# Weight, activation and S slots of a two-block transformer kernel moved to other byte places in SBUF

## The chip, the cores and the metric

The kernel runs on one core of one Trainium2 chip. The metric is the device time of one execution in microseconds (us); of several runs the median is given.

## What is computed

Two transformer blocks run one after the other on one sequence of 256 tokens, D = 1024, in fp32. The first has two layers, a differential attention and a stick-breaking attention, each followed by a sparse "PEER" layer. The second has four layers (sparse-index attention, sliding window, latent attention, sparse-index attention), each followed by an MLP with squared ReLU. What matters here is the PEER layer and the MLP:

```python
def _peer(x, w_pq, sub_keys, u, v):
    ...
    q = (xt @ w_pq).reshape(T, PEER_HEADS, 2, PEER_HALF)
    scores = jnp.einsum('thcd,hckd->thck', q, sub_keys)
    ...
    def block(args):
        xblk, idb, gb = args
        u_sel = jnp.take(u, idb, axis=0)
        h = jax.nn.gelu(jnp.einsum('td,ted->te', xblk, u_sel), approximate=False)
        v_sel = jnp.take(v, idb, axis=0)
        return jnp.einsum('te,ted->td', gb * h, v_sel)

def sqrelu_mlp(h, w_up, w_down):
    return jnp.square(jax.nn.relu(h @ w_up)) @ w_down
```

The 16384 experts are not gathered: the kernel multiplies with all of `u` and all of `v`, and a dense matrix of gates, zero for experts that were not chosen, lies between the two.

## The kernel before

**Chunks.** All weights come as 932 chunks of 128 partitions x 1024 fp32 (4096 bytes a partition), in the order of `stream_plan`. `Stream._load` fetches a chunk into one of three `raw` tiles (a DMA on SP's queue, line 106). `Stream._fill` splits it into two parts: ScalarE writes the rounded high part `whi` (line 134), VectorE, and for some chunks GpSimd, the rest `wlo` (line 136). Activations are split the same way. A product of fp32 precision is then three matmuls: high x high, high x low, low x high, all through the helper `mm` (line 229).

**Places.** A slot's place is its start in bytes within a partition of SBUF. The slots of `whi` and `wlo` come from a base pool with 4 of each, used in turn, and in most stages from a second, lent pool of 5 to 7 of each. A slot has 1040 elements = 4160 bytes, of which 4096 are used, so neighbouring slots differ by 64 bytes modulo 512. The four base slots of `whi` start at bytes 30720, 43200, 39040 and 34880 in the order of use, those of `wlo` at 47360, 59840, 55680 and 51520. Modulo 512 that is (0, 256), (192, 448), (128, 384) and (64, 320) for the pairs (`whi`, `wlo`). The activations `hT` (two tiles of `Parts`, 8192 bytes each) and the S parts share two places, 64000 and 72192, both 0 modulo 512. Inside all of these tiles an operand of a matmul starts at a multiple of 512 bytes from the tile's start, so the two numbers of a pair are the distances, modulo 512, from the activation's operand to the weight's operand.

**The sparse layer** (`peer`, layers 0 and 1). First 128 chunks of `peer_u`: per chunk 24 matmuls of 256 columns into `ps_h` (`fm_products`), with the weights as the stationary operand (`LDWEIGHTS`) and `hT` moving. In the shadow of these, VectorE selects experts (`select`) and TensorE, VectorE and ScalarE build the gates (`gate`, `ps_g`). Then 128 chunks of `peer_v`: per chunk 12 matmuls of 512 columns into `acc` (`acc_rows`), with S parts stationary and the weights moving; `split_s` makes the S parts, one pair of 8192 bytes for four chunks. Chunks of `peer_u` and the first 70 of `peer_v` use base slots alone; later ones a lent pool too.

**The MLPs** (`mlp`, four of them): 32 pairs of an `up` chunk (24 matmuls of 256 columns into `ps_fm`) and a `dn` chunk (12 of 512 into `acc`), with base and lent slots. In the long middle part of an MLP both kinds of chunk lie in the 7 lent slots in turn.

The order of instructions is set by a scheduler that places recorded instructions on each engine. Between the sparse layer and the mixer before it, GpSimd's queue issues three DMAs: two that save `x` to DRAM (`x_dram`, line 737) and one that loads the sub-keys (`peer_keys`, line 774) into the tile `Xb`.

Of the kernel before, what the change touches and what calls it, by code (L numbers as in the profile page):

```python
# [11 lines left out]
F32R = mybir.dt.float32r  # L12
# [7 lines left out]
P = 128  # L20
D = 1024
S = 256
ND = 8
NEG = -1.0e30
SLOT = 1040
ALPHA = 4.0 ** 0.25
LAMBDA_INIT = 0.8 - 0.6 * math.exp(0.0)
N_KEYS = 128
# [55 lines left out]
class Stream:  # L84
# [7 lines left out]
    def __init__(self, tc, plan, find, raw, parts):  # L92
# [5 lines left out]
        self.raws, self.done = {}, {}  # L98
        self.loaded = self.split = self.pos = 0

    def _load(self):
        c = self.loaded
        src = self.find(*self.plan[c])
        n = src.shape[-1]
        t = self.raw_pool.tile([P, 1024], F32, tag="raw", name=f"raw{c}")
        self.nc.sync.dma_start(t[:, :n], src)
        self.raws[c] = (t, n)
        self.loaded += 1
# [7 lines left out]
    def _fill(self, last):  # L116
        last = min(last, len(self.plan) - 1)
        while self.split <= last:
            c = self.split
            pool = self._slot(c)  # L120
            if pool is None:
                return
            pool[2].append(c)
            if c not in self.raws:
                self._load()
            t, n = self.raws.pop(c)
            hi = pool[0].tile([P, SLOT], F32R, tag="whi", name=f"whi{c}")[:, :1024]
            lo = pool[0].tile([P, SLOT], F32R, tag="wlo", name=f"wlo{c}")[:, :1024]
            name, g = self.plan[c]
            lo_eng = self.nc.gpsimd if name in POOL_LO and g in POOL_LO[name] else self.nc.vector  # L130
            if name in DVE_HI:
                self.nc.vector.tensor_copy(hi[:, :n], t[:, :n])
            else:
                self.last_hi = self.nc.scalar.copy(hi[:, :n], t[:, :n])  # L134
            with self.tc.issue_after(self.behind) if self.n_behind and lo_eng is self.nc.vector else nullcontext():
                lo_eng.tensor_tensor(lo[:, :n], t[:, :n], hi[:, :n].bitcast(F32), ALU.subtract)  # L136
            self.n_behind = max(self.n_behind - 1, 0)
            self.done[c] = (hi, lo)
            self.split += 1
            while self.loaded < min(self.split + self.N_RAW, len(self.plan)):  # L140
                self._load()
# [35 lines left out]
def tile_two_blocks(ctx: ExitStack, tc: tile.TileContext, t: dict, out: bass.AP, dbg=None):  # L177
# [5 lines left out]
    xt_pool = ctx.enter_context(tc.tile_pool(name="xt_pool", bufs=2))  # L183
# [53 lines left out]
    class Parts:  # L237


        def __init__(self):  # L240
            self.t = [xt_pool.tile([P, 4, 2, 2, P], F32R, tag="xt", name=f"hT{i}") for i in range(2)]

        def hi(self, d):
            return self.t[d // 4][:, d % 4, :, 0, :]
# [114 lines left out]
    def lend(px, bufs, *names):  # L359

        st.lend(px.enter_context(tc.tile_pool(name="lent", bufs=bufs)), bufs, names)
        px.callback(st.take_back)
# [4 lines left out]
    def new_accs():  # L367
        return [halves(a2.tile([P, 2, 512], F32, tag="a2", name=f"acc{tt}")) for tt in range(2)]
# [290 lines left out]
    def stick_breaking(hT):  # L659
        with ExitStack() as px:  # L660
            k1 = px.enter_context(tc.tile_pool(name="k1", bufs=1))
            sp = px.enter_context(tc.tile_pool(name="sp", bufs=2))
            lend(px, 6, "b_v", "b_kq", "b_wo")
            smask = k1.tile([P, 384], F32, name="smask")
            seg = k1.tile([P, 768], F32, name="seg")
            nc.gpsimd.dma_start(smask, t["k_smask"])
            nc.gpsimd.dma_start(seg, t["k_seg"])
            lng = bcast(k1, t["ln_g"][2], D, "lng")
            lnb = bcast(k1, t["ln_b"][2], D, "lnb")
            v_sb = k1.tile([P, 2, D], F32, name="v_sb")  # L670
            accs = new_accs()
            ch = [(("b_v", d), lambda tt, part, d=d: hT.one(d, tt, part)) for d in range(8)]
            acc_rows(ch[:4], accs, True, 1)
            for d in range(4, 8):
                acc_rows([ch[d]], accs, False, stop=d == 7)
            for tt in range(2):
                nc.scalar.copy(half(v_sb[:, tt], 0), accs[tt][0])
                nc.vector.tensor_copy(half(v_sb[:, tt], 1), accs[tt][1])
            oT = new_oT(k1)
            stt = {}  # L680

            def stage_p(g):
                res = []
                for i in range(2):
                    ps = proj_fm(hT, "b_kq", 2 * g + i)
                    r = sp.tile([P, S], F32, tag=f"raw{i}", name="kq")
                    nc.scalar.copy(r, ps[:, :S])
                    res.append(r)
                stt[g] = res

            def stage_l(g):
                kr, qr = stt.pop(g)
                ps = logits_pair(lambda h: qr[h * 64 : h * 64 + 64, :], lambda h: kr[h * 64 : h * 64 + 64, :])
                z = sp.tile([P, 768], F32, tag="z", name="z")
                zv = z.rearrange("p (a b) -> p a b", a=2)
                nc.vector.scalar_tensor_tensor(
                    zv, ps[:, :, :384], 0.125, smask.unsqueeze(1).to_broadcast([P, 2, 384]), ALU.mult, ALU.add
                )
                e = sp.tile([P, 768], F32, tag="e", name="e")
                nc.scalar.activation(e, z, AF.Abs)  # L700
                nc.scalar.activation(e, e, AF.Exp, scale=-1.0)
                nc.scalar.activation(e, e, AF.Ln, bias=1.0)
                nc.vector.scalar_tensor_tensor(e, z, 0.0, e, ALU.max, ALU.add)
                c = sp.tile([P, 768], F32, tag="c", name="c")
                nc.vector.tensor_tensor_scan(c[:, ::-1], seg[:, ::-1], e[:, ::-1], 0.0, ALU.mult, ALU.add)
                nc.vector.tensor_tensor(z, z, c, ALU.subtract)
                nc.scalar.activation(z, z, AF.Exp)
                stt[g] = zv

            def stage_t(g):  # L710
                zv = stt.pop(g)
                pTs = transposes_pair(zv, sp)
                ps = ms.tile([P, 512], F32, tag="ms", name="ps_av")
                for h in range(2):
                    f = slice(g * P + h * 64, g * P + h * 64 + 64)
                    o = ps[h * 64 : h * 64 + 64]
                    mm(o[:, :S], v_sb[:, 0, f], pTs[:, h, : 2 * P], start=True)
                    mm(o[:, P:S], v_sb[:, 1, f], pTs[:, h, 2 * P :], stop=True)
                pe["behind"] = pe["last"]
                copy_parts(ps[:, :S], g, oT)  # L720

            for s in range(8 + 2):
                if s < 8:
                    stage_p(s)
                if 0 <= s - 1 < 8:
                    stage_l(s - 1)
                if 0 <= s - 2 < 8:
                    stage_t(s - 2)
            nT = Parts()
            acc_wo("b_wo", oT, lambda tt, acc: to_hT(x[:, tt, :], tt, nT, norm_residual(tt, acc, lng, lnb, sp)))  # L730
            return nT


    def peer(layer, hT, last):
# [5 lines left out]
        with ExitStack() as px:  # L740
# [218 lines left out]
            def split_s(b):  # L959
                src = Xa[:, 4 * b : 4 * b + 4, :] if b < NA else Xb[:, 4 * b - J1 : 4 * b - J1 + 4, :]  # L960
                for n in range(2 if b >= NA else 0):
                    hb = ab.tile([P, 2, S], F32, tag="hs", name="hb")
                    nc.gpsimd.dma_start(hb, h_dram[(4 * b - J1) // 2 + n])
                    nc.vector.tensor_tensor(src[:, 2 * n : 2 * n + 2], src[:, 2 * n : 2 * n + 2], hb, ALU.mult)
                if b < NB - 2:
                    sh = xt_pool.tile([P, 2, 4, S], F32R, tag="xt", name="S_parts")
                    hi, lo = sh[:, 0], sh[:, 1]
                elif b == NB - 2:
                    hi, lo = (ab.tile([P, 4, S], F32R, tag="AB", name="S_parts") for _ in range(2))
                else:  # L970
                    hi, lo = (own["k1"].tile([P, 4, S], F32R, name=f"S_last{i}") for i in range(2))
                nc.scalar.copy(hi, src)
                dve_sub_lo(lo, src, hi)
                return [
                    ((f"peer_v{layer}", b * 4 + i), lambda tt, part, i=i: (hi, lo)[part][:, i, tt * P : (tt + 1) * P])
                    for i in range(4)
                ]
# [16 lines left out]
            nT = None  # L994
# [591 lines left out]
    hT = Parts()  # L1586
# [3 lines left out]
    hT = diff_attention(hT)  # L1590
    dump(0)
    hT = peer(0, hT, False)
    dump(1)
    hT = stick_breaking(hT)
    dump(2)
    hT = peer(1, hT, True)
    dump(3)
    mixers = [lambda h: dsa(0, 0, h), lambda h: swa(1, h), lambda h: mla(2, h), lambda h: dsa(1, 3, h)]
    for i in range(4):
        hT = mixers[i](hT)  # L1600
        dump(4 + 2 * i)
        hT = mlp(i, *hT)
# [136 lines left out]
```

## Time and profile before

| | |
|---|---|
| median of 3 runs | 3140.53 us (3134.71 to 3141.01) |
| the profiled execution | 3139.05 us, of which the span of its instructions 3137.3 us |
| TensorE busy | 3023.1 us (96%), mean granted clock 0.984 of full speed |
| VectorE, ScalarE, GpSimd busy | 2081.8, 1666.3, 316.6 us |
| `peer_u` of layer 0, of layer 1 | 206.4 to 627.2, 1157.0 to 1578.0 us |
| `peer_v` of layer 0, of layer 1 | 627.3 to 990.2, 1578.0 to 1943.0 us |
| the four MLPs | 185.8, 187.1, 187.7 and 184.4 us |

A trace lists each instruction with its start. Matmuls are pipelined, so a matmul's own duration (0.28 us for 256 columns) spans several that run behind it; the pace is read from start to start.

### The profile page before, as it was taken

To read this page: it belongs to the slowest core of one execution; us is meant where nothing else is said; L and a number is where in the kernel's file an instruction comes from. 1 tells how busy PE (TensorE), PEld (TensorE's weight loads), DVE (VectorE), ACT (ScalarE), POOL (GpSimd) and SP (SyncE) were. 2 spreads that over 40 slices of the span, in tenths; PEclk is the share of its full clock that TensorE was granted. 3 is DMA by queue.
4 is the path that set the end of the run, shared out by engine and by line. 5 is a ranking of instruction groups with operands and counts; after the bars stand their busy time and mean duration, and the time that the engine had idled before them with its cause. 6 is when DMAs were issued, how large, how long until landed. Compare 5 with 4: busy or idle time off the path is not lost.

```text
span 3137.3 us, 51266 instructions
## 1 busy us (share of the span) xinstructions
PE 3023.1 (96%) x19968; PEld 2720.8 (87%) x19968; DVE 2081.8 (66%) x3603; ACT 1666.3 (53%) x2844; POOL 316.6 (10%) x246
## 2 busy tenths in 40 slices
PE   8699999999999899999999999999999989999999
PEld 6599999978887789999988887889889968998898
DVE  5479867775555769957766555865566566556654
ACT  5434568744443634568744444554555455554553
POOL 1410000010001310000010002400120021003200
PEclk9899999999999999999999999999999999999999
DMA  6855555576655435555576654445526532554364
GB/s 201 134 161 184 184 189 169 169 265 205 223 189 183 146 122 182 180 191 169 169 258 211 229 191 159 150 162 188 184 78 217 189 110 98 194 189 143 125 201 135
DMA packets 157636, 551.05 MB, mean 176 GB/s; under 512 B 18880, under 2 KB 19712, under 8 KB 157392
## 3 DMA queue, kind: packets, MB, share of 16 engines
q1 hardware_dynamic: 135216, 489.42, 47.0%
q0 software_dynamic: 12112, 41.54, 5.3%
q10 hardware_dynamic: 10064, 16.81, 1.5%
q8 instruction: 157, 2.57, 0.3%
q14 instruction: 87, 0.71, 0.1%
HBM read 523.59 MB, written 24.10 MB: 175 GB/s over the span
## 4 chain that ended last, share of the span: by engine, by line
PE 79%; DMA 8%; DVE 5%; ACT 3%; issue 2%; POOL 1%; SPq 0%; ACTq 0%; DVEq 0%; POOLq 0%
PE acc L229 31%; PE ps_h L229 23%; PE ps_fm L229 17%; PE ps_g L229 4%; DMA hb<-h_dram 3%; DVE wlo L136 1%; ACT whi L134 1%; PE ps_av L229 1%; PE ps_l L229 1%; POOL wlo L136 1%; DMA raw<-in_a_wo_dram 1%; DMA raw<-in_dsa_in_dram 1%; DMA raw<-in_peer_q_dram 1%; PE ps_pT L456 1%; DMA raw<-in_b_kq_dram 1%
## 5 line engine op out<-in xcount | busy, mean ns | idle before, releaser
L134 ACT CAST whi<-raw 128x1024 fp32r<-128x1024 f32 (+1 forms) x908 | 948.0, 1046 | 1007.9 <-PE acc L229 279.3
L136 DVE TENSOR_TENSOR wlo<-raw,whi 128x1024 fp32r<-128x1024 f32 (+1 forms) x854 | 1043.0, 1225 | 606.6 <-ACT whi L134 602.7
L229 PE MATMUL ps_h<-hT,whi 128*128 128x256 f32 x4096 | 733.5, 281 | 0.0
L229 PE MATMUL ps_fm<-hT,whi 128*128 128x256 f32 x3424 | 659.9, 286 | 13.5 <-DVE hT L235 4.1
L229 PEld LDWEIGHTS ps_h<-hT,whi 128*128 128x128 f32 x4096 | 628.2, 189 | 1.0
L229 PEld LDWEIGHTS ps_fm<-hT,whi 128*128 128x128 f32 x3424 | 555.1, 191 | 33.1 <-DVE hT L235 5.3
L229 PE MATMUL ps_h<-hT,wlo 128*128 128x256 f32 x2048 | 577.6, 282 | 0.0
L229 PE MATMUL acc<-whi,S_parts 128*128 128x512 f32 x1984 | 539.8, 393 | 0.0
L229 PE MATMUL ps_fm<-hT,wlo 128*128 128x256 f32 (+1 forms) x1936 | 529.3, 283 | 0.0
L229 PEld LDWEIGHTS acc<-whi,S_parts 128*128 128x128 f32 x1984 | 372.6, 188 | 86.0
L229 PEld LDWEIGHTS ps_h<-hT,wlo 128*128 128x128 f32 x2048 | 386.9, 189 | 0.2
L229 PEld LDWEIGHTS ps_fm<-hT,wlo 128*128 128x128 f32 (+1 forms) x1936 | 369.1, 191 | 1.3 <-issue 0.5
L229 PE MATMUL acc<-wlo,S_parts 128*128 128x512 f32 x992 | 310.3, 394 | 4.3 <-DVE wlo L136 4.3
L136 POOL TENSOR_TENSOR wlo<-raw,whi 128x1024 fp32r<-128x1024 f32 (+1 forms) x78 | 196.0, 2524 | 1042.7 <-ACT whi L134 967.1
L229 PEld LDWEIGHTS acc<-wlo,S_parts 128*128 128x128 f32 x992 | 185.8, 188 | 48.8 <-DVE wlo L136 6.3
L229 PE MATMUL acc<-whi,hh 128*128 128x512 f32 x512 | 162.9, 394 | 0.0
L229 PE MATMUL acc<-wlo,hh 128*128 128x512 f32 x512 | 162.6, 393 | 0.0
L229 PE MATMUL acc<-whi,hl 128*128 128x512 f32 x512 | 162.0, 393 | 0.0
L892 DVE TENSOR_SCALAR AB<-iota,selT 128x128 f32<-128x128 f32 x512 | 141.7, 340 | 12.4 <-PE ps_g L229 11.9
L229 PE MATMUL acc<-whi,oT 128*128 128x512 f32 x384 | 128.9, 419 | 11.8 <-ACT oT L482 9.2
L896 ACT ACTIVATE AB<-iota,selT 128x128 f32<-128x128 f32 x384 | 122.9, 391 | 30.0 <-PE ps_g L229 29.4
L229 PE MATMUL ps_g<-AB 128*128 128x128 f32 x1024 | 133.5, 275 | 0.0
(353 smaller groups left out, 3192.7 us busy)
## 6 DMA issues: line engine op xcount, KB each, us to landing
raw<-in_peer_u_dram SPq DMA_DIRECT2D x256, 512.0 KB, 3.7
raw<-in_peer_v_dram SPq DMA_DIRECT2D x256, 512.0 KB, 4.3
raw<-in_up_dram SPq DMA_DIRECT2D x128, 512.0 KB, 4.2
raw<-in_dn_dram SPq DMA_DIRECT2D x128, 512.0 KB, 4.2
raw<-in_dsa_in_dram SPq DMA_DIRECT2D x30, 512.0 KB, 4.2
h_dram<-hs ACTq DMA_DIRECT2D x56, 256.0 KB, 2.2
hb<-h_dram POOLq DMA_DIRECT2D x56, 256.0 KB, 3.7
raw<-in_a_qk_dram SPq DMA_DIRECT2D x16, 512.0 KB, 4.3
```

The lines of the kernel that those rows point to most:

```text
L134: self.last_hi = self.nc.scalar.copy(hi[:, :n], t[:, :n])
L136: lo_eng.tensor_tensor(lo[:, :n], t[:, :n], hi[:, :n].bitcast(F32), ALU.subtract)
L229: pe["last"] = nc.tensor.matmul(o, lhsT, rhs, start=start, stop=stop)
L456: nc.tensor.transpose(pT[:, h, b * P : (b + 1) * P], p_sb[:, h, b * P : (b + 1) * P], ident)
L892: nc.vector.tensor_scalar(A[:, i], iota, selT[:, 0, tk : tk + 1], selT[:, 2, tk : tk + 1], ALU.is_equal, ALU.mult)
L896: nc.scalar.activation(B[:, i], iota, AF.Abs, bias=selT[:, 1, tk : tk + 1], scale=-1.0)
```

## The change

The slots get other places; no instruction is added or taken away.

- A base slot has 1088 elements = 4352 bytes (17 x 256), a lent slot 1024 = 4096 bytes, a tile of `hT` or S 2112 elements = 8448 bytes (33 x 256).
- In `peer_u0` and `peer_v1` the weights of chunk g begin 16 x (g mod 16) bytes into their base slots, `whi` and `wlo` alike.
- The `hT` that the stick-breaking layer leaves for sparse layer 1 begins 64 bytes into its tiles (`Parts(16)`).
- The S parts of group b in `peer_v` of layer 0 begin 16 x (b mod 16) bytes into theirs.
- Everything else that is stationary or moving in these stages starts where its slot starts.

The resulting tiles of `hT` start at bytes 65536 and 73984, 0 and 256 modulo 512. The base slots start at 30720, 43776, 39424 and 35072 (`whi`) and 48128, 61184, 56832 and 52480 (`wlo`): 0, 256, 0 and 256 for both parts. In `peer_u0` the distances of both parts are thus equal, and run through all multiples of 16; in `peer_u1` they are 192 or 448 for both parts in every chunk. In the first three MLPs the lent slots of both parts lie at 128, in the fourth at 0, and `hh`, `hl` lie at the same place modulo 512 as the `dn` weights.

```diff
-SLOT = 1040
+SLIDE = 64
...
+    def slide(self, key):
+
+        name, g = key
+        return 4 * (g % 16) if name in ("peer_u0", "peer_v1") else 0
...
-            hi = pool[0].tile([P, SLOT], F32R, tag="whi", name=f"whi{c}")[:, :1024]
-            lo = pool[0].tile([P, SLOT], F32R, tag="wlo", name=f"wlo{c}")[:, :1024]
+            base = pool is self.pools[0]
+            width = 1024 + (SLIDE if base else 0)
+            at = self.slide(self.plan[c]) if base else 0
+            hi = pool[0].tile([P, width], F32R, tag="whi", name=f"whi{c}")[:, at : at + 1024]
+            lo = pool[0].tile([P, width], F32R, tag="wlo", name=f"wlo{c}")[:, at : at + 1024]
...
-        def __init__(self):
-            self.t = [xt_pool.tile([P, 4, 2, 2, P], F32R, tag="xt", name=f"hT{i}") for i in range(2)]
+        def __init__(self, at=0):
+            whole = [xt_pool.tile([P, 2048 + SLIDE], F32R, tag="xt", name=f"hT{i}") for i in range(2)]
+            self.t = [
+                w[:, at : at + 2048].rearrange("p (d a b t) -> p d a b t", d=4, a=2, b=2) for w in whole
+            ]
...
-            nT = Parts()
+            nT = Parts(16)
             acc_wo("b_wo", oT, lambda tt, acc: to_hT(x[:, tt, :], tt, nT, norm_residual(tt, acc, lng, lnb, sp)))
...
-                    sh = xt_pool.tile([P, 2, 4, S], F32R, tag="xt", name="S_parts")
+                    at = 4 * (b % 16) if layer == 0 else 0
+                    sh = xt_pool.tile([P, 2048 + SLIDE], F32R, tag="xt", name="S_parts")
+                    sh = sh[:, at : at + 2048].rearrange("p (a b t) -> p a b t", a=2, b=4)
```

On TensorE, VectorE, ScalarE and SP the order of the instructions is word for word what it was. On GpSimd one DMA of each sparse layer stands elsewhere. Before, at the start of sparse layer 0 (`Xb` is the tile that takes the sub-keys, `x_dram` the copy of `x` in DRAM, the `wlo` rows split chunks of `peer_q0`):

```order
L136 TENSOR_TENSOR wlo_1426<-raw_1411,whi_1425 128x1024
L136 TENSOR_TENSOR wlo_1432<-raw_1417,whi_1431 128x1024
L774 DMA Xb<-in_peer_keys_dram 128x1024
L737 DMA x_dram<-x 128x1024
L136 TENSOR_TENSOR wlo_1608<-raw_1423,whi_1607 128x1024
L136 TENSOR_TENSOR wlo_1614<-raw_1429,whi_1613 128x1024
L737 DMA x_dram<-x 128x1024
```

And in the changed kernel, at the same place of the same queue:

```order
L144 TENSOR_TENSOR wlo_1426<-raw_1411,whi_1425 128x1024
L144 TENSOR_TENSOR wlo_1432<-raw_1417,whi_1431 128x1024
L748 DMA x_dram<-x 128x1024
L144 TENSOR_TENSOR wlo_1608<-raw_1423,whi_1607 128x1024
L144 TENSOR_TENSOR wlo_1614<-raw_1429,whi_1613 128x1024
L748 DMA x_dram<-x 128x1024
L785 DMA Xb<-in_peer_keys_dram 128x1024
```

The load of the sub-keys now stands behind both saves of `x`; the same happens at the start of sparse layer 1.

## Rows read from the trace of the kernel before

**Rows 1.** The page: busy time by engine, and the chain that ended last.
```profile
PE 3023.1 (96%) x19968; PEld 2720.8 (87%) x19968; DVE 2081.8 (66%) x3603; ACT 1666.3 (53%) x2844; POOL 316.6 (10%) x246
...
PE 79%; DMA 8%; DVE 5%; ACT 3%; issue 2%; POOL 1%; SPq 0%; ACTq 0%; DVEq 0%; POOLq 0%
```

**Rows 2.** Busy time in stretches: `peer_u0`, `peer_v0`, the first MLP.
```profile
core 0: us, PE busy (x) PEld busy (x) DVE busy (x) ACT busy (x) POOL busy (x), PEclk, DMA share, GB/s
206.40:627.20 420.80, 420.80 (x3632) 419.80 (x3630) 346.76 (x822) 267.34 (x469) 0.55 (x1) 1.00 0.54 178
627.30:990.20 362.90, 358.47 (x1545) 290.12 (x1544) 215.30 (x195) 170.88 (x169) 27.51 (x35) 1.00 0.65 215
2058.80:2244.60 185.80, 184.75 (x1193) 167.06 (x1192) 114.91 (x144) 98.62 (x150) 10.60 (x5) 1.00 0.59 193
```

**Rows 3.** Timeline of PE in `peer_u0`: the first matmuls of five chunks on end.
```profile
294.34 0.40 PE L229 MATMUL ps_h<-hT,whi 128*128 128x256 f32 x2
...
297.22 0.39 PE L229 MATMUL ps_h<-hT,whi 128*128 128x256 f32 x2
...
299.94 0.39 PE L229 MATMUL ps_h<-hT,whi 128*128 128x256 f32 x2
...
302.78 0.40 PE L229 MATMUL ps_h<-hT,whi 128*128 128x256 f32 x2
...
305.52 0.40 PE L229 MATMUL ps_h<-hT,whi 128*128 128x256 f32 x2
```

**Rows 4.** Timeline of PE in `peer_v0`: the first low-part matmuls of five chunks.
```profile
666.64 0.62 PE L229 MATMUL acc<-wlo,S_parts 128*128 128x512 f32 x2
...
669.39 0.63 PE L229 MATMUL acc<-wlo,S_parts 128*128 128x512 f32 x2
...
672.18 0.63 PE L229 MATMUL acc<-wlo,S_parts 128*128 128x512 f32 x2
...
674.97 0.62 PE L229 MATMUL acc<-wlo,S_parts 128*128 128x512 f32 x2
...
677.73 0.39 PE L229 MATMUL acc<-wlo,S_parts 128*128 128x512 f32 x1
```

**Rows 5.** Timeline of PE in the first MLP: an `up`, a `dn`, and later `up` chunks.
```profile
2142.83 0.41 PE L229 MATMUL ps_fm<-hT,whi 128*128 128x256 f32 x2
...
2145.67 0.62 PE L229 MATMUL acc<-whi,hh 128*128 128x512 f32 x2
...
2148.45 0.28 PE L229 MATMUL ps_fm<-hT,whi 128*128 128x256 f32 x1
...
2182.11 0.41 PE L229 MATMUL ps_fm<-hT,whi 128*128 128x256 f32 x2
```

**Rows 6.** Timeline of PE in the first attention: one chunk of `a_qk`, first and last.
```profile
80.45 0.40 PE L229 MATMUL ps_fm<-hT,whi 128*128 128x256 f32 x2
...
83.17 0.28 PE L229 MATMUL ps_fm<-hT,wlo 128*128 128x256 f32 x1
```

**Rows 7.** The tile `whi`: durations in ns, min/median/max, of the two splitting instructions.
```profile
L134 ACT CAST whi<-raw x908: 822/1049/1061, 7.0 to 3114.3; 128x1024 fp32r<-128x1024 f32 x180, 128x832 fp32r<-128x832 f32 x1, 128x768 fp32r<-128x768 f32 x1
L136 DVE TENSOR_TENSOR wlo<-raw,whi x854: 949/1224/2524, 8.1 to 3115.4; 128x1024 fp32r<-128x1024 f32 x170, 128x768 fp32r<-128x768 f32 x1
```

**Rows 8.** Timeline of POOL: the second saves of `x`; then the sub-keys' landing times.
```profile
183.28 0.56 POOL L737 DMA_DIRECT2D x_dram<-x  x1 [1.50 <-DVE x L401]
...
1133.97 0.57 POOL L737 DMA_DIRECT2D x_dram<-x  x1 [1.51 <-DVE x L401]
...
DMA to landing us min/median/max: 4.1/4.6/5.1
```

**Rows 9.** Timeline of PE: the first readers of the sub-keys, layers 0 and 1.
```profile
195.52 0.49 PE L229 MATMUL ps_sc<-Xb 64*128 64x128 f32 x2
...
1146.22 0.48 PE L229 MATMUL ps_sc<-Xb 64*128 64x128 f32 x2
```

## The prediction

> **What bounds the kernel now.** I read the page first: TensorE is busy 96% of the span and holds 79% of the chain that ended last [rows 1]. [...] So the question is whether the pace depends on where the operands lie, which only the timeline tells.
>
> It does. Five chunks of `peer_u0` on end run the same 24 matmuls on the same `hT`, and start 2.88, 2.72, 2.84 and 2.74 us apart [rows 3]. Their slots are, in that order, (0, 256), (192, 448), (128, 384) and (64, 320): the two at an odd multiple of 64 bytes are the quick ones. The fifth chunk is back in the first slot, and the round of four is 11.18 us, 116.5 ns a matmul. In `peer_v0` the chunks' starts differ less, 2.75, 2.79, 2.79 and 2.76 us, 11.09 us a round [rows 4].
>
> [...]
>
> **The change, part by part.**
>
> *`peer_u0`, 128 chunks, weights sliding by 16 bytes.* Two things change: the distance from activation to weight runs through all multiples of 16, and the low part, which lay 256 bytes (modulo 512) from the high part, now lies at the same distance as it. The second matters, since the MLP has chunks of that kind. Its chunk at 2142.83 us has both parts at 192, and takes 2.84 us [rows 5], not the 2.72 of the pair (192, 448). So of every 16 chunks I give the two at 64 and 192 the 2.84 us of that row. The two at 0 and 128 have no such row; their nearest are the slots at 0 and 128 with 2.88 and 2.84, so 2.86. The other twelve lie off the multiples of 64. Nearest is a chunk of `a_qk` with its parts at 224 and 160, odd multiples of 32: 2.72 us from its first to its last matmul, 23 steps, or 118.3 ns each, 2.84 us for 24 [rows 6]. That value mixes: (2 x 2.84 + 2 x 2.86 + 12 x 2.84)/16 = 2.84 us, a round of four 11.37 instead of 11.18 us. Over 32 rounds that is 0.19 x 32 = 6 us more.
>
> *`peer_u1`, `hT` shifted by 64 bytes.* Every chunk now has both parts at 192 for one half of its matmuls and at 448 for the other: 2.84 us by the MLP's chunk [rows 5], again 11.36 a round, 0.18 x 32 = 5.8 us more.
>
> From these 12 us I take off a third. The quick slots reach their pace only after some matmuls, and in the second half of both stages the gate's matmuls (3632 matmuls ran in the stretch, 3072 are the chunks') [rows 2] cut in and break it off, so the old rounds were slower there than 11.18. I take **+8 us** for both. The bounds are the quickest and the slowest chunk throughout: 4 x 2.72 = 10.88 gives 64 x (-0.30) = -19 us, 4 x 2.88 = 11.52 gives 64 x 0.34 = +22 us. They would both need all 16 places of `peer_u0` to be of one kind, which four places of three kinds in rows 3 make unlikely.
>
> *`peer_v`, 256 chunks.* Its stretches now spread over many distances. Chunks range from 2.75 to 2.79 us, and the average of the old places is 2.77 [rows 4]. I take 2.78 for a wider mixture, 0.01 x 256 = **+2 us**, with -5 us if all were at 2.75 and +5 at 2.79.
>
> *The MLPs, 128 pairs.* Seven pairs take 2182.11 - 2142.83 = 39.28 us, 5.61 each [rows 5]. Now the `up` weights lie at 128 or 384 of `hT` (0 or 256 in the fourth MLP) in both parts, the `dn` weights at 0 of `hh`. `up`: 2.84 to 2.88 us by rows 3 and 5. `dn`: 2.78 in the row [rows 5]; at distance 0 nearest is `peer_v`'s slot (0, 256), 2.75, at worst 2.79. The sum is 5.59 to 5.67; I take 5.61, so **0 us**, and keep 128 x (-0.02) = -3 and 128 x 0.06 = +8 us.
>
> *The mixers* have the same moves on a path that other engines set as well; they are short, and I take 0, with 2 us either way.
>
> *ScalarE and VectorE* write to the new places. Over all places of before, odd multiples of 32 bytes among them, a cast has a median of 1049 and a maximum of 1061 ns; the subtraction's median is 1224 ns on VectorE [rows 7]. There is no second level at some of the places, and both engines are less busy than TensorE (346.76 and 267.34 of 420.80 us [rows 2]): 0 us. The DMAs write `raw`, whose places stay.
>
> *The sub-keys' load* moves behind the second save of `x` on GpSimd's queue. That save is issued at 183.28 us and takes 0.56; the load's issue, taken to be as long, ends at 184.4, and the load lands at most 5.1 us later [rows 8], at 189.5 us. Its first reader is TensorE at 195.52 [rows 9]: 6 us of cover. In layer 1 the save at 1133.97 makes it 1140.2 against 1146.22. Nothing else is queued on GpSimd until the `hb` loads of `peer_v`. 0 us; without the cover TensorE would stand for what is late.
>
> Sum: 8 + 2 + 0 = +10 us on the profiled execution's 3139.05 us, **3149 us**. That execution lies 1.5 us under the median of the runs, inside their spread of 6 us. The forecast's own band is 3141 to 3159: the `peer_u` term between 4 and 13, `peer_v` and MLPs within their bounds but not all at one end.
>
> **The rivals.**
>
> *The distance alone decides, and odd multiples of 64 bytes are quick (faster).* Then `peer_u1`, with every chunk at 192 or 448, would run at the 2.72 to 2.74 us of the two quick slots: 4 x 2.73 = 10.92, 0.26 x 32 = -8 us. `peer_u0` would mix as before, the MLPs' `dn` at distance 0 gives -3, `peer_v` up to -2: -13 us, 3126 us. For it: both quick slots of rows 3 are of this kind. Against it: the MLP's chunk, both parts at 192 and 2.84 us [rows 5]. The point is whether a low part 256 bytes away from the high one is needed for 2.72 us. 16%.
>
> *The place of the weights alone decides, or equal parts at even multiples are the worst.* `peer_u1`'s weights lie at 0 and 256, whatever `hT` does; the slot at 0 takes 2.88 us [rows 3], 0.34 x 32 = +11 us, and `peer_u0`'s +6 stays. With the MLPs' `up` at 2.88 (+5) the time is 3139 + 22 = 3161 us. For it: in all rows of before `hT` lies at 0, so distance and place can't be told apart. 12%.
>
> *No net effect.* The new mixture of places has the same mean as the old one, 3139 us, 3133 to 3144. [...] For it: `peer_u`'s four slots have their mean between the two kinds, and so would a random set of places. 22%.
>
> [...]
>
> **How the numbers follow.** The forecast has 50%, the rivals 16, 12 and 22%. A measurement of this kernel can tell about 0.2%, 6 us, from no change. Of the forecast's 50 about 40 lie above that; with the 12 of the second rival, slower has 0.52. Same has 18 of the no-effect rival's 22, 9 of the forecast's and 2 of the first rival's, 0.29. Faster has the rest, 0.19. The range of 8 in 10 goes from 3128, which leaves out the larger part of the first rival, to 3163, which takes in the second.
>
> **What would show it.** Right: `peer_u1`'s chunks start 2.84 us apart in all four slots, and its stretch grows by 4 to 6 us over 421.0; `peer_u0`'s chunks differ with a period of 16, the mean at 2.84; splitting instructions take as long as before; the sub-keys land before 190 us. Wrong: chunks of `peer_u1` at 2.73 us or below (first rival), at 2.88 (second), any `peer_u0` chunk far outside 2.72 to 2.88, a `dn` chunk over 2.80, or idle time of TensorE ahead of `ps_sc`.

## The result, and the profile after

The changed kernel takes 3157.51 us (median of 4 runs, 3154.86 to 3159.99), the kernel before, measured beside it, 3140.77 us (4 runs, 3134.71 to 3145.27). The ratio is 1.0054, with a 95% interval of 1.0035 to 1.0074: slower, by 16.7 us. The forecast was slower by 10 us, 3149, with a range of 3128 to 3163. A second measurement on another chip, told below, gave a smaller ratio, 1.0028 [1.0014, 1.0043]. The profiled execution of the changed kernel took 3158.58 us, with a span of 3156.8 us, against 3139.05 and 3137.3 before.

The page of the changed kernel, busy time and the chain that ended last:

```profile
PE 3035.6 (96%) x19968; PEld 2735.7 (87%) x19968; DVE 2084.3 (66%) x3603; ACT 1666.7 (53%) x2844; POOL 317.2 (10%) x246
...
PE 79%; DMA 8%; DVE 6%; ACT 3%; issue 2%; POOL 1%; DVEq 0%; ACTq 0%; SPq 0%; POOLq 0%
```

Against [rows 1] TensorE is busy 12.5 us longer (3035.6 against 3023.1) with the same 19968 matmuls; VectorE differs by 2.5 us, ScalarE by 0.4. The chain's shares are the same but for VectorE's (6% against 5%). So most of the added time is matmuls that take longer, and the question is in which stages, and whether by their places or by the clock. Busy time in stretches of the changed kernel, columns as in [rows 2]: `peer_u0`, `peer_v0`, `peer_u1`, the first MLP.

```profile
206.90:632.10 425.20, 425.20 (x3632) 424.19 (x3631) 346.90 (x820) 267.02 (x469) 0.55 (x1) 1.00 0.53 176
632.20:996.80 364.60, 358.78 (x1546) 290.44 (x1545) 215.70 (x195) 170.89 (x169) 27.49 (x35) 1.00 0.65 214
1161.70:1585.40 423.70, 423.70 (x3632) 422.68 (x3631) 346.74 (x821) 267.01 (x469) 0.55 (x1) 1.00 0.53 176
2069.30:2255.60 186.30, 185.32 (x1193) 168.50 (x1192) 112.93 (x144) 98.59 (x150) 10.90 (x5) 1.00 0.59 192
```

`peer_u0` is still never idle and still at the full clock, 1.00, but takes 425.20 us instead of 420.80 [rows 2]; `peer_u1` takes 423.70 with the same 3632 matmuls. Taken from the first matmul of a stage to the first of the next, all stages of both profiled executions compare so:

| us | before | after | difference | forecast |
|---|---|---|---|---|
| `peer_u0` | 420.90 | 425.27 | +4.4 | +8 for both |
| `peer_u1` | 420.90 | 423.74 | +2.8 | |
| `peer_v`, both layers | 728.34 | 730.91 | +2.6 | +2 |
| four MLPs | 745.33 | 748.98 | +3.6 | 0 |
| mixers and the rest | 807.40 | 813.80 | +6.4 | 0 |
| all | 3122.87 | 3142.69 | +19.8 | +10 |

All of the +6.4 us in the last line but one is one stage, the latent attention: 75.12 us before, 81.50 after. The part on where the prediction failed shows that it goes with the granted clock, 0.93 over this stage before and 0.85 after.

The timeline of PE in `peer_u0` of the changed kernel shows how the sliding places differ. These are the first matmuls of chunks whose weights lie 48, 64, 80 and 96 bytes (modulo 256) behind `hT`; a chunk's time is the step to the next row:

```profile
310.41 0.40 PE L237 MATMUL ps_h<-hT,whi 128*128 128x256 f32 x2
...
313.24 0.39 PE L237 MATMUL ps_h<-hT,whi 128*128 128x256 f32 x2
...
315.96 0.40 PE L237 MATMUL ps_h<-hT,whi 128*128 128x256 f32 x2
...
318.81 0.40 PE L237 MATMUL ps_h<-hT,whi 128*128 128x256 f32 x2
```

The chunk at 48 takes 2.83 us, the one at 64 takes 2.72 and the one at 80 takes 2.85. Of the 16 places 64 alone is that quick: chunks away from the gate's matmuls take 2.87 at 0, 2.88 at 112, 128 and 160, 2.80 at 208 and 224, and 2.81 to 2.87 at the others. In `peer_u1`, with `hT` shifted by 64 bytes, all four slots take the same time:

```profile
1256.28 0.40 PE L237 MATMUL ps_h<-hT,whi 128*128 128x256 f32 x2
...
1259.11 0.40 PE L237 MATMUL ps_h<-hT,whi 128*128 128x256 f32 x2
...
1261.93 0.40 PE L237 MATMUL ps_h<-hT,whi 128*128 128x256 f32 x2
...
1264.76 0.40 PE L237 MATMUL ps_h<-hT,whi 128*128 128x256 f32 x2
```

2.83, 2.82 and 2.83 us, and 2.83 for the fourth, which ends at 1267.59, where before the four slots took 2.88, 2.72, 2.84 and 2.74 [rows 3]. In the first MLP of the changed kernel an `up` chunk, a `dn` chunk and the next `up` start at:

```profile
2125.39 0.40 PE L237 MATMUL ps_fm<-hT,whi 128*128 128x256 f32 x2
...
2128.26 0.63 PE L237 MATMUL acc<-whi,hh 128*128 128x512 f32 x2
...
2131.03 0.40 PE L237 MATMUL ps_fm<-hT,whi 128*128 128x256 f32 x2
```

That is 2.87 and 2.77 us, 5.64 a pair, against 5.61 [rows 5]. The moved load of the sub-keys has all the cover it was given. The timeline of the changed kernel has the second save, the load's issue, and the first reader:

```profile
183.22 0.58 POOL L748 DMA_DIRECT2D x_dram<-x  x1 [1.51 <-DVE x L412]
183.80 0.54 POOL L785 DMA_DIRECT2D Xb<-in_peer_keys_dram  x1
...
195.75 0.48 PE L237 MATMUL ps_sc<-Xb 64*128 64x128 f32 x2
```

Its issue begins at 183.80 and it lands at most 5.2 us later by the load's view, at 189.0: the reader at 195.75 does not wait for it [rows 8, 9]. In layer 1 it begins at 1138.91 and lands by 1144.1, ahead of a reader at 1150.67. And the two splitting instructions on the tile `whi` take what they took by their medians, 1047 and 1225 ns against 1049 and 1224 [rows 7]:

```profile
L142 ACT CAST whi<-raw x908: 824/1047/1062, 7.0 to 3134.3; 128x1024 fp32r<-128x1024 f32 x180, 128x832 fp32r<-128x832 f32 x1, 128x768 fp32r<-128x768 f32 x1
L144 DVE TENSOR_TENSOR wlo<-raw,whi x854: 949/1225/2392, 8.1 to 3135.3; 128x1024 fp32r<-128x1024 f32 x170, 128x768 fp32r<-128x768 f32 x1
```

### The profile page after: what moved, and what is told of

The parts are those of the page before. It is cut to its first block, busy times and chain, and to the rows that moved or that the text cites. A ratio compares the mean times of both kernels' runs of the same rounds, so it can differ in the third digit from the quotient of the medians.

```text
span 3156.8 us, 51266 instructions
## 1 busy us (share of the span) xinstructions
PE 3035.6 (96%) x19968; PEld 2735.7 (87%) x19968; DVE 2084.3 (66%) x3603; ACT 1666.7 (53%) x2844; POOL 317.2 (10%) x246
## 4 chain that ended last, share of the span: by engine, by line
PE 79%; DMA 8%; DVE 6%; ACT 3%; issue 2%; POOL 1%; DVEq 0%; ACTq 0%; SPq 0%; POOLq 0%
PE acc L237 32%; PE ps_h L237 23%; PE ps_fm L237 16%; PE ps_g L237 4%; DMA hb<-h_dram 3%; DVE wlo L144 1%; ACT whi L142 1%; PE ps_av L237 1%; PE ps_l L237 1%; POOL wlo L144 1%; DMA raw<-in_a_wo_dram 1%; DMA raw<-in_dsa_in_dram 1%; PE ps_xT L274 1%; DMA raw<-in_peer_q_dram 1%; PE ps_pT L467 1%
## 5 line engine op out<-in xcount | busy, mean ns | idle before, releaser
L237 PE MATMUL acc<-whi,oT 128*128 128x512 f32 x384 | 128.2, 417 | 12.5 <-ACT oT L493 9.4
```

What stands on the lines that cost most here:

```text
L237: pe["last"] = nc.tensor.matmul(o, lhsT, rhs, start=start, stop=stop)
```

## The experiments

Below, the distance of a chunk is the place of its weights minus the place of its activations, modulo 256 bytes. Chunk times are steps between first matmuls, in the first half of a stage, where no gate cuts in.

**(a) Parts that do not shift.** `hT` of sparse layer 1 goes back to 0; everything else is the changed kernel.

```diff
-            nT = Parts(16)
+            nT = Parts()
```

> The changed kernel, with the activations of sparse layer 1 at the start of their tiles again. If the distance from activation to weight sets the pace: peer_u1's distances become 0 and 256 for both parts in every chunk, as in chunks 0, 16, 32 of peer_u0, so its chunks go from 2.83 to 2.87 us and its stretch grows by 5 us. If the weights' own place sets it: the weights stay where they were, 2.83 us and no change. If the 6 us that the latent attention took longer in the changed kernel are tied to places, they are here again; if they are an accident of one execution, the stage is back near 75 us.

Measured: 3165.98 us in one run, 3143.9 before (23 runs, 3133.59 to 3152.24). Every chunk of `peer_u1` that nothing cuts into takes 2.88 us (1268.20, 1271.08 and 1273.96 are the starts of three on end) and the stage 429.73 us, 6.0 more than in the changed kernel. The weights lie at the same places in both. So the place of the weights does not set the pace by itself: distance 0 costs 2.88, distance 192 costs 2.83.

**(b) The two parts of a chunk at equal places.** The kernel before, with its low parts' base slots moved by 768 bytes, so that both parts of a chunk lie at one and the same of 0, 192, 128 and 64 (modulo 512).

```diff
-    parts_pool = ctx.enter_context(tc.tile_pool(name="parts_pool", bufs=4))
+    hi_pool = ctx.enter_context(tc.tile_pool(name="hi_pool", bufs=4))
+    ctx.enter_context(tc.tile_pool(name="pad1", bufs=1)).tile([P, 192], F32, name="pad1")
+    lo_pool = ctx.enter_context(tc.tile_pool(name="lo_pool", bufs=4))
```

> The kernel before, with the low parts' base slots moved by 768 bytes, so that both parts of a chunk lie at the same distance: (0, 0), (192, 192), (128, 128), (64, 64). If the distance between the parts matters: 2.87, 2.83, 2.88 us for the first three, 2.72 to 2.84 for the fourth, a round of 11.30 to 11.42 in place of 11.18, 4 to 8 us more for each peer_u stretch. If the high part's distance alone decides: 2.88, 2.72, 2.84, 2.74 us as before, and no change.

Measured: 3144.58 us in one run, 3143.9 before. The timeline of PE in its `peer_u0`, first matmuls of five chunks:

```profile
295.83 0.40 PE L234 MATMUL ps_h<-hT,whi 128*128 128x256 f32 x2
...
298.71 0.39 PE L234 MATMUL ps_h<-hT,whi 128*128 128x256 f32 x2
...
301.44 0.40 PE L234 MATMUL ps_h<-hT,whi 128*128 128x256 f32 x2
...
304.28 0.40 PE L234 MATMUL ps_h<-hT,whi 128*128 128x256 f32 x2
...
307.01 0.28 PE L234 MATMUL ps_h<-hT,whi 128*128 128x256 f32 x1
```

2.88, 2.73, 2.84 and 2.73 us, the steps of [rows 3] within 0.01, and a stage of 420.89 us against 420.90. Whether the low part lies 256 bytes from the high one or not changes nothing. So 256 bytes make no difference here, places can be counted modulo 256, and the reason on which the prediction's `peer_u` term rests is gone.

**(c) All base slots at distance 64.** The kernel before, with base slots 4096 bytes apart, behind pads, so that all lie at 64 or 320 (modulo 512).

```diff
+    ctx.enter_context(tc.tile_pool(name="pad0", bufs=1)).tile([P, 16], F32, name="pad0")
...
+            width = BASE_SLOT if pool is self.pools[0] else SLOT
```

(`BASE_SLOT` is 1024 elements; `SLOT`, 1040, stays for the lent pools.)

> The kernel before, with all base slots at one pair of distances, (64, 320), that of its quick fourth slot. If the distances set the pace: every peer_u chunk takes 2.72 to 2.74 us, a round 10.9, each peer_u stretch is 8 us shorter, each peer_v stretch up to 2 us, the kernel 16 to 20 us faster than before. If the quick slot is quick because of the slots used before and after it: 2.8 us each, no change.

Measured: 3132.58 us (12 runs, 3127.95 to 3139.5) against 3143.9, ratio 0.9967 [0.9956, 0.9978]. The timeline of PE in its `peer_u0`:

```profile
302.14 0.39 PE L235 MATMUL ps_h<-hT,whi 128*128 128x256 f32 x2
...
304.86 0.39 PE L235 MATMUL ps_h<-hT,whi 128*128 128x256 f32 x2
...
307.58 0.39 PE L235 MATMUL ps_h<-hT,whi 128*128 128x256 f32 x2
```

2.72 us in every slot, and stages of 415.58 and 416.03 us. With the same instructions in the same order, places alone make the kernel 11 us faster: the pace hangs on where the two operands lie (2.72 us a chunk here, 2.88 at distance 0 [rows 3]), whatever the reason.

The gain is less than expected, 5.3 and 4.9 us a stage and not 8, 11 us in all and not 16 to 20. One reason is that TensorE, never idle in this stage before, now is. The stretch of `peer_u0`, columns as in [rows 2]:

```profile
208.20:623.70 415.50, 412.77 (x3632) 410.99 (x3631) 346.65 (x821) 266.66 (x469) 0.56 (x1) 1.00 0.57 180
```

It stands for 2.7 us. For both `peer_u` stages together the page of this run has 3.4 us of idle time before matmuls into `ps_h` that VectorE ended and 0.7 us that ScalarE ended; VectorE has as much to do as before (346.65 us against 346.76 in `peer_u0`). Another reason is told with the experiment on the order.

**(f) Lent slots alone.** The kernel before with the lent slots at the changed kernel's width, base slots as they were.

```diff
+            width = SLOT if pool is self.pools[0] else 1024
```

> The kernel before, with lent slots alone 4096 bytes wide as in the changed kernel; base slots, activations and S as before. If the MLPs' and mixers' part of the loss comes from the lent slots' places: the four MLPs together 3 to 4 us longer, and the latent attention 6 us longer, 9 us in all. If the mixers' part was an accident of one execution: 3 to 4 us in all, the latent attention within 2 us of 75.

Measured: 3146.65 us (10 runs, 3143.0 to 3154.21) against 3143.9, ratio 1.0015 [1.0004, 1.0026]. The sparse layers stay (420.89, 420.90, 727.85 us), the MLPs take 748.05 us, 2.7 more, by chunks of 2.876 and 2.764 us as in the changed kernel. So the lent slots alone cost the MLPs 2.7 us. The latent attention takes 74.62 us.

**(g, h) `hT` shifted in the kernel before, twice.** First by 64 bytes in layer 0 and 128 in layer 1; then by 192 and 32. The weights' four places stay. The `S_parts` tiles are wider too, with their parts at 0.

```diff
-            nT = Parts()
+            nT = Parts(16)
...
-            nT = Parts()
+            nT = Parts(32)
```

> The kernel before, with the activations of sparse layer 0 moved by 64 bytes and those of layer 1 by 128; the weights' slots stay. In the order of the places 0, 192, 128, 64 the four base slots took 2.88, 2.72, 2.84, 2.74 us. If the distance modulo 256 alone decides: with 64, distances 192, 128, 64, 0, so 2.72, 2.84, 2.74, 2.88; with 128, distances 128, 64, 0, 192, so 2.84, 2.74, 2.88, 2.72. If the weights' place alone decides: 2.88, 2.72, 2.84, 2.74 in both layers. If both places count on their own: the slot at 0 takes 2.83 with 64, as in the changed kernel's peer_u1, and neither row of four comes out whole.

The second has 48 and 8 elements in these two places.

> As the last, with 192 bytes in layer 0 and 32 in layer 1. Distance alone: with 192, distances 64, 0, 192, 128, so 2.74, 2.88, 2.72, 2.84; with 32, distances 224, 160, 96, 32, which peer_u0 of the changed kernel showed at 2.80, 2.88, 2.81, 2.84. The weights' place alone: 2.88, 2.72, 2.84, 2.74 in both layers.

Measured: 3151.38 and 3157.92 us, one run each, 3147.36 before (13 runs, 3137.72 to 3151.84). The timeline of PE in `peer_u0` of the first, chunks with weights at 0, 192, 128, 64 and again 0:

```profile
297.15 0.39 PE L230 MATMUL ps_h<-hT,whi 128*128 128x256 f32 x2
...
299.87 0.40 PE L230 MATMUL ps_h<-hT,whi 128*128 128x256 f32 x2
...
302.71 0.40 PE L230 MATMUL ps_h<-hT,whi 128*128 128x256 f32 x2
...
305.45 0.40 PE L230 MATMUL ps_h<-hT,whi 128*128 128x256 f32 x2
...
308.33 0.28 PE L230 MATMUL ps_h<-hT,whi 128*128 128x256 f32 x1
```

2.72, 2.84, 2.74 and 2.88 us. The slot at 0, the slowest in [rows 3], is now the quickest, at distance 192, and the slot at 64 is the slowest, at distance 0. Its layer 1, 128 bytes off, gives 2.84, 2.74, 2.88 and 2.72 us, as the distances 128, 64, 0 and 192 have it. In the second kernel they move on: 0 takes 2.74 (distance 64), 192 takes 2.88 (distance 0). In its layer 1, 32 bytes off, the four distances 224, 160, 96 and 32 take 2.80, 2.87, 2.82 and 2.83 to 2.84 us, as the places 224, 160, 96 and 32 do in `peer_u0` of the changed kernel (2.80, 2.88, 2.81, 2.84). So in these four stages the distance modulo 256 counts, wherever the two operands lie; the second rival's reason, the place of the weights, is refuted.

One thing fits no rule of distance alone: at 192 these chunks take 2.72 us, in `peer_u1` of the changed kernel 2.83. The experiment on the order, below, is about that.

**(i) All slots at 64.** The kernel with all base slots at 64, and now the lent slots, `S_parts` and the MLPs' hidden parts at 64 (modulo 256) as well, by pads ahead of the lent pools and `S_parts` 64 bytes into their tiles. `hT` stays at 0, so the matmuls of 256 columns (`peer_u`, `up`) have distance 64, those of 512 (`peer_v`, `dn`) distance 0.

```diff
-            width = BASE_SLOT if pool is self.pools[0] else SLOT
+            width = BASE_SLOT
...
-                    lend(px, 5, f"peer_v{layer}")
+                    lend(px, 5, f"peer_v{layer}", pad=(48, 32)[layer])
```

> The kernel with all base slots at (64, 320), and also all lent slots of the sparse layers and the MLPs at 64 modulo 256, the S parts and the MLPs' hidden parts at 64 as well, the activations at 0. If equal places of S parts and weights give 2.72 us a peer_v chunk, as at distances 0 and 16 in the changed kernel's peer_v0: 13 us less in the two peer_v stretches than before. If an up chunk at distance 64 takes 2.72 us as in peer_u: the MLPs 14 us less; if 2.83 as the lent slots with both parts at 64 did: 0 to 3 us less. With peer_u's 10 us: 23 to 37 us under the kernel before. If the pace hangs on something else than these places, peer_v and the MLPs stay at 728 and 745 us.

Measured: 3119.83 us (6 runs, 3114.45 to 3122.91) against 3147.36, ratio 0.9914 [0.9898, 0.9931]. This beats both kernels. `peer_v` falls to 725.07 us for both layers and the MLPs to 738.41. The timeline of PE, three low-part matmuls of `peer_v0`, and an `up`, a `dn` and an `up` of the first MLP:

```profile
646.56 0.62 PE L235 MATMUL acc<-wlo,S_parts 128*128 128x512 f32 x2
...
649.28 0.62 PE L235 MATMUL acc<-wlo,S_parts 128*128 128x512 f32 x2
...
2100.86 0.40 PE L235 MATMUL ps_fm<-hT,whi 128*128 128x256 f32 x2
...
2103.68 0.62 PE L235 MATMUL acc<-whi,hh 128*128 128x512 f32 x2
...
2106.40 0.40 PE L235 MATMUL ps_fm<-hT,whi 128*128 128x256 f32 x2
```

`peer_v` runs at 2.72 us a chunk where it took 2.75 to 2.79 [rows 4], and `dn` at 2.72 where it took 2.78 [rows 5]. But `up`, at the same distance 64 as `peer_u`, takes 2.82, not 2.72. And of the 13 us that were expected of `peer_v` only 3.3 came. The stretch of `peer_v0`, columns as in [rows 2]:

```profile
624.40:984.10 359.70, 352.92 (x1546) 289.80 (x1544) 215.19 (x195) 170.74 (x169) 27.46 (x35) 1.00 0.67 217
```

TensorE is busy 5.6 us less than in [rows 2] (352.92 against 358.47), but idle for 6.8 us, which was 4.4: here too a quicker pace is in part spent on waiting.

**The changed kernel once more**, nothing edited, on the chip of g, h and i.

> The changed kernel once more, unaltered. If the 6 us in the latent attention were an accident of the profiled execution, the stage takes 75 to 77 us here, and peer_u, peer_v and the MLPs repeat their 849.0, 730.9 and 749.0 us within 1 us; the kernel is then some 11 to 15 us slower than before, not 17. If they are tied to places: 81 us again.

Measured: 3155.82 us (8 runs, 3152.11 to 3166.49) against 3147.36, ratio 1.0028 [1.0014, 1.0043]. `peer_u0` and `peer_u1` take 425.20 and 423.73 us, as the first time; `peer_v` takes 733.26 us and the MLPs 750.00, more than the 1 us allowed for `peer_v`; the latent attention takes 81.29, which is what was expected if it were tied to places. More on that below. The two ratios differ mostly because the kernel before took 3140.77 us there and 3147.36 here.

**(k) Layer 1 at distance 64 in the changed kernel.** `hT` shifted by 192 bytes instead of 64.

```diff
-            nT = Parts(16)
+            nT = Parts(48)
```

> The changed kernel, with the activations of sparse layer 1 moved by 192 bytes in place of 64: all peer_u1 chunks at distance 64 in place of 192. If the distance modulo 256 sets the pace: 2.72 us each, and the peer_u1 stretch is 416 in place of 424 us, the kernel 8 us faster than the changed one. If chunks with both parts at the same distance can't be quick, or the place 0 of the weights holds them back: 2.83 us, 424 us.

Measured: 3152.45 us (10 runs, 3142.14 to 3158.77) against 3144.91 (17 runs, 3137.82 to 3151.2), ratio 1.0027 [1.0015, 1.0039]. The chunks of `peer_u1` take 2.72 us (starts at 1262.91, 1265.63, 1268.35) and the stage 415.67, 8.1 us less than with a shift of 64. In the whole kernel's time these 8 us can't be told: the ratio is 1.0027, that of the changed kernel 1.0054 and 1.0028, each on another chip. By distance 64 and 192 are mirror images; with every chunk alike, 64 is quick here (2.72 us) and 192 slow in `peer_u1` of the changed kernel (2.83 us).

**(l) The same four distances in another order.** The kernel before with base slots 128 bytes wider (not 64, as the expectation says), so that chunks come at 0, 64, 128, 192 instead of 0, 192, 128, 64.

```diff
+            width = 1072 if pool is self.pools[0] else SLOT
```

> The kernel before, with base slots 64 bytes wider, so that the same four distances come in the order 0, 64, 128, 192 and not 0, 192, 128, 64. Distance 192 has shown two paces: 2.72 us right after a chunk at 0, 2.83 after 192 or 176. If a chunk's pace hangs on the chunk ahead too: 192, now behind 128, takes 2.83 us, and 64, now behind 0, may leave its 2.74; a round is 11.2 to 11.4 us. If the distance alone decides: 2.88, 2.74, 2.84, 2.72, a round of 11.18.

Measured: 3161.03 us in one run, 3144.91 before. The timeline of PE in its `peer_u0`, chunks at 0, 64, 128, 192 and again 0:

```profile
295.34 0.40 PE L230 MATMUL ps_h<-hT,whi 128*128 128x256 f32 x2
...
298.21 0.40 PE L230 MATMUL ps_h<-hT,whi 128*128 128x256 f32 x2
...
301.04 0.40 PE L230 MATMUL ps_h<-hT,whi 128*128 128x256 f32 x2
...
303.89 0.40 PE L230 MATMUL ps_h<-hT,whi 128*128 128x256 f32 x2
...
306.71 0.28 PE L230 MATMUL ps_h<-hT,whi 128*128 128x256 f32 x1
```

2.87, 2.83, 2.85 and 2.82 us; no quick chunk is left in these rows (some at 64 elsewhere in the stage take 2.73). Both `peer_u` stages take 425.1 us instead of 420.9. Same distances, same work, another order: what ran ahead counts. All runs together give, for a chunk of 24 matmuls behind a whole chunk:

| distance | chunk ahead | us | seen in |
|---|---|---|---|
| 0 | 0, 64, 192 or 240 | 2.87 to 2.89 | before, after, a, g, h, l |
| 128 | 64 or 192 | 2.84 to 2.85 | before, l, g, h |
| 128 | 112 | 2.88 | after |
| 64 | 128, 48 or 64 | 2.72 to 2.74, rarely 2.83 | before, after, g, h, c, k, i |
| 64 | 0, or a `dn` chunk | 2.83, rarely 2.73 | l, i |
| 192 | 0 | 2.72 to 2.73 | before, g, h |
| 192 | 128, 176 or 192 | 2.83 | l, after |

("after" is the changed kernel.) At 0 there is nearly one pace; at 128 there are 2.84 and 2.88, at 64 and 192 2.72 and 2.83.

The distance of the chunk ahead is not all that counts. In the kernel c every chunk lies at 64, and still two whole chunks on end in its `peer_u0` take 2.83 and 2.82 us, not 2.72:

```profile
352.51 0.40 PE L235 MATMUL ps_h<-hT,whi 128*128 128x256 f32 x2
...
355.34 0.40 PE L235 MATMUL ps_h<-hT,whi 128*128 128x256 f32 x2
...
358.16 0.40 PE L235 MATMUL ps_h<-hT,whi 128*128 128x256 f32 x2
```

Ahead of them a matmul of the gate (`ps_selT`, at 351.52) cut into a chunk, for which TensorE had stood 1.2 us. The chunk's matmuls start 113 and 114 ns apart before the cut and 117 to 119 behind it, and so they go on until the next cut, at 358.75; a little later they are back at 113 and 114. So the two paces are two rhythms, 113 to 114 and 117 to 119 ns a matmul, that last from chunk to chunk at one and the same distance; a matmul in between switched them here, and with another order of distances a chunk at 192 took 2.82 us instead of 2.72.

**(n) An `up` at distance 224.** In the kernel with all slots at 64 `up` is slow behind `dn`; here its `hT` moves by 96 bytes, and 224 is a distance with 2.80 us.

```diff
-        nT = Parts()
+        nT = Parts(24)
```

> The kernel with all weights, S and hidden parts at 64, and the MLPs' activations moved by 96 bytes, so that up chunks lie at distance 224 in place of 64. If the distance sets the pace there as in peer_u (2.80 us at 224): up chunks go from 2.83 to 2.80 us, the MLPs together 3 us shorter, at 735 us. If behind a dn chunk every distance gives 2.83 us or more: 738 us, no change.

Measured: 3120.82 us (6 runs, 3115.4 to 3131.91) against 3144.91, ratio 0.9922 [0.9907, 0.9937]; the MLPs take 740.95 us, no less than 738.41; 2.1 of the 2.5 us more lie in the third MLP, of which more below. The timeline of PE in the first MLP, an `up`, a `dn`, an `up`:

```profile
2104.24 0.40 PE L235 MATMUL ps_fm<-hT,whi 128*128 128x256 f32 x2
...
2107.05 0.63 PE L235 MATMUL acc<-whi,hh 128*128 128x512 f32 x2
...
2109.79 0.28 PE L235 MATMUL ps_fm<-hT,whi 128*128 128x256 f32 x1
```

`up` takes 2.81 here (2.80 over the stage) instead of 2.82, but `dn`, whose own distance is still 0, takes 2.74 instead of 2.72. A pair is 5.546 us against 5.547. What one chunk gains the next gives back.

## Why the prediction was right in sign, and where it failed

**`peer_u`: right size, wrong reason.** +8 us were forecast, +7.2 came. The places of `peer_u0` mix to a mean of 2.84 us a chunk (forecast 2.84), and all slots of `peer_u1` take 2.83. Over 128 chunks each at these paces the stages would grow by 5.3 + 4.1 = 9.4 us; 2.2 of them do not come, where the prediction took off a third of 12 for the gate's matmuls. They do break off a quick pace, as the part on the order shows (2.83 and 2.82 us behind the cut in kernel c, not 2.72). In the kernel before, the quick slot at 192 has its pace from its first matmul (112 to 114 ns from start to start in the chunk at 297.22 [rows 3]) and the one at 64 after three (117, 123 and 118 ns at first in the chunk at 302.78); in the chunk at 438.67, right behind a cut of the gate, the slot at 192 runs at 117 to 120 ns to its end, 2.83 us. `peer_u1` grew by 2.8 us, not by the 4 to 6 that were named as a sign. But the failed step is "The second matters, since the MLP has chunks of that kind": the low part lying 256 bytes from the high one was held to be needed for 2.72 us, and the experiment with equal parts shows the same 2.88, 2.73, 2.84 and 2.73 us without it. The MLP's chunk at 2142.83 [rows 5], with both parts at 192, was read as slow for its parts; the order experiment shows that a chunk at 64 or 192 has two paces, 2.72 and 2.83 us, and that what ran ahead decides, and the MLP's chunk stands behind a `dn`. `peer_u1` of the changed kernel has each chunk at 192 behind one at 192, and every one of them that nothing cuts into runs at the slow pace, 2.83 us. So the analogue gave the right duration, by luck.

**The first rival**, that distance alone decides and odd multiples of 64 are quick, was nearer to the cause: distance counts, and with `peer_u` all at 64 nearly every chunk that nothing cuts into is quick. What it lacked is the order; by it `peer_u1` would have run at 2.73, and it ran at 2.83. **The second**, the place of the weights, is refuted by the two shifts of `hT`. Its other half, that distances 0 and 128 are slow, holds (2.88, and 2.84 to 2.88), but the change put few `peer_u` chunks there: two of 16 in `peer_u0`, none in `peer_u1`; the MLPs' `up` lies there, see below. **No net effect** is refuted by 1.0054 [1.0035, 1.0074] and 1.0028 [1.0014, 1.0043], and its reason, that the new mixture of places has the mean of the old one, by `peer_u0`, which is never idle in either kernel and takes 425.20 us against 420.80 [rows 2]. How far places alone move the time shows kernel i, 0.9914 [0.9898, 0.9931].

**`peer_v`**: +2 forecast, +2.6 came. In `peer_v0` of the changed kernel chunks take 2.72 us where the S parts and the weights lie at equal places or 16 bytes apart, up to 2.81 elsewhere. For these matmuls of 512 columns distance 0 is thus quick, not slow, where the chunks around lie alike; the slot at 0 in the kernel before took 2.75.

**The MLPs: a term mis-sized.** 5.61 us a pair were taken, 0 us in all. The pair takes 5.64 in the first three MLPs and 5.62 in the fourth: `up` 2.876, inside "2.84 to 2.88", and `dn` 2.764, inside 2.75 to 2.79. The bounds held, but the middle of them, 5.63, was passed over for 5.61, the old time. What the places cost is the +2.7 us of the lent slots alone (f). The +3.6 of the profiled execution is not the same thing: 2.7 of it lie in the third MLP, in the kernel before and in the changed one:

```profile
2645.80:2833.70 187.90, 186.34 (x1185) 169.09 (x1186) 110.36 (x138) 95.02 (x142) 7.86 (x3) 0.98 0.58 190
```

```profile
2661.70:2852.20 190.50, 187.61 (x1184) 170.82 (x1185) 110.64 (x138) 95.07 (x142) 7.97 (x3) 0.98 0.57 187
```

Half of that is idle time (2.9 us against 1.6), and the third MLP took 191.45 us in g too, whose MLPs have the places of before, but 188.64 and 188.56 in a and k, which have the new ones. At the same distance 0 `dn` takes 2.72 us behind an `up` at 64, 2.74 behind one at 224 and 2.76 here behind one at 128: what ran ahead counts for it too.

**The mixers: a term mis-sized, and not by the places.** 0 was taken, +6.4 came, all of it in the latent attention. Its stretch in the kernel before, in the changed kernel, and in the one with unshifted parts, which has the changed kernel's places there, columns as in [rows 2]:

```profile
2534.10:2609.20 75.10, 59.65 (x353) 51.76 (x351) 57.12 (x134) 49.13 (x138) 22.75 (x15) 0.93 0.34 106
```

```profile
2543.30:2624.80 81.50, 63.62 (x355) 56.56 (x353) 58.58 (x134) 49.82 (x138) 22.80 (x15) 0.85 0.32 97
2592.00:2608.00 16.00, 11.85 (x53) 11.32 (x54) 8.86 (x19) 8.72 (x23) 7.07 (x3) 0.57 0.34 109
```

```profile
2558.90:2634.50 75.60, 59.86 (x354) 52.41 (x353) 57.17 (x134) 49.43 (x138) 22.64 (x15) 0.91 0.35 105
```

In the last two the places are the same, and the stage takes 81.5 or 75.6 us. In the changed kernel's long one the granted clock is 0.85 over the stage and 0.57 in 16 us of it, 0.50 in 13.6 us of these (from 2594.2 to 2607.8 us); TensorE was busy 11.85 of these 16 us. In the short ones the clock is 0.93 and 0.91 over the stage. Over all profiled executions the stage has two lengths: 74.6 to 77.8 us, at a clock of 0.91 to 0.93, in before and in a, b, c, f, g and k, and 81.2 to 81.6, at 0.85 to 0.87, in both of the changed kernel and in h, i, l and n. So the length goes with the clock. Places do not fix it, since a and k have the changed kernel's places there and are short (75.66 and 75.88 us). Whether the long one comes by chance is not shown: both executions of the changed kernel that were profiled have it, and why the clock falls for longer in one execution than in another stays open. Without the stage the profiled difference is 13.1 us, made of terms that the forecast had at 10.

**ScalarE, VectorE and the sub-keys**: 0 forecast, and nothing found in their medians and in the first reader's start, by the rows above.

## What to carry to other kernels

Where TensorE never idles and the granted clock is 1.00, look at the starts of like chunks on end: if the same matmuls take different times from slot to slot (here 2.72 to 2.88 us), the distance in bytes between the stationary and the moving operand, modulo 256, is worth a look, and so is the order in which such distances follow each other. Here constant places (distance 64 for matmuls of 256 columns, 0 for those of 512), made by pads of a few elements, took 0.9% off a tuned kernel with no instruction changed, while a sliding place averaged the good places away. Count on less than the pace promises: at the quick places TensorE began to wait (2.7 us in `peer_u0` of kernel c, where it was never idle before), and 8 us a stage became 5. A number that comes out right is no proof of its reason: the test that mattered was the one that changed the supposed cause alone and moved nothing.

## What the runs showed of the hardware that was not expected

- The pace of a matmul of 256 columns lies between 2.72 and 2.89 us for 24, or 113.3 to 120 ns each in the mean, by the distance of its operands modulo 256 bytes and by what ran ahead. For 512 columns it is 2.72 to 2.82 us for 12, 226.7 to 235 ns each in the mean. No run has a chunk under 2.72.
- At distances 64 and 192 matmuls of 256 columns have two paces, 2.72 and 2.83 us a chunk, and what ran ahead decides: 420.9 us a stage in one order, 425.1 in another. At 64 either can last over several chunks (352.51 to 358.16 us in kernel c, and the rows at 302.14).
- What in the memory or in TensorE's reads makes these paces, and what is carried from one chunk to the next, no run shows; the runs only show on which distances and orders they depend. Nor is it shown why the clock gives the latent attention two lengths.
